# The recurrent branch of a two-layer block on one core: where the projection work stands among its products, and which engine does its elementwise passes

## The chip, the cores and the metric

One core of a Trainium2 chip runs the whole program. The metric is the time of one execution on the device in microseconds: the median of three runs of the kernel before is 2986.39 us (2982.87 to 2990.86).

## The reference

Two layers of a transformer block over 256 context and 256 latent tokens, width 1024. The normed tokens `h` go through one wide projection `w_in`, which feeds three branches and their gates: latent attention, neighbourhood attention, and a recurrence. Layer 0 ends in a dense feed-forward, layer 1 in a mixture of eight experts. The change concerns the recurrence alone, 8 heads of 64, once forward and once backward in time:

```python
w_log = -jax.nn.softplus(-(w0 + jnp.einsum('bldr,drc->bldc', jnp.tanh(wd), w2))) - 0.5
decay = jnp.exp(-jnp.exp(w_log))
a = jax.nn.sigmoid(a0 + jnp.einsum('bldr,drc->bldc', ad, a2))
kk = to_heads(k * k_k, RW_HEADS)
kk = kk / jnp.maximum(jnp.sqrt(jnp.sum(kk * kk, axis=-1, keepdims=True)), 1e-12)
k_dir = k[:, :, None, :] * (1.0 + (a - 1.0) * k_a)
def step(S, inp):
    r_t, w_t, k_t, v_t, kk_t, a_t = inp
    sa = jnp.einsum('bhij,bhj->bhi', S, -kk_t)
    S = S * w_t[:, :, None, :] + sa[..., None] * (kk_t * a_t)[:, :, None, :] + v_t[..., None] * k_t[:, :, None, :]
    return S, jnp.einsum('bhij,bhj->bhi', S, r_t)
bonus = (jnp.sum(r[:, :, None] * k_dir * r_k, axis=-1, keepdims=True) * v[:, :, None]).sum(axis=2)
```

## The kernel before

The projection `w_in` is 57 tiles of up to 128 columns. Each tile is 24 products on TensorE: eight slices of the depth, and for each three products of split operands (`mm3`, L314, L315, L316), 512 tokens wide or 256 where only the latent tokens count. A tile's weights come by DMA, ScalarE rounds them (`whi`, L469) and GpSimd takes the remainder (`wlo`, L470), in two passes of 512 columns for a tile. The generator `serve` gives this work out a slice at a time; the same stream carries the modulation products (L339) of the next layer.

`weave` runs the recurrence and, at each of its `yield w`, draws about `w` microseconds of projection from `serve`. The numbers in `K.W` so say how much projection is laid in at which point. What the recurrence leaves over is drawn later, in the attention. After that a scheduler orders each engine's instructions; each engine then runs its own list in order. The names below are those of the code.

The recurrence of a layer is two halves of four heads, one after the other, each in these steps (`rw_half`):

- **Front** (`rw_front`): the norm of `kk` through two products (L562, L572), a square root on ScalarE and a reciprocal on VectorE. The second half's front stands inside the first half's chain.
- **Preparation**: four rounds (two head pairs, two directions). A round has two products from the low-rank inputs (L609, L614), two tanh and two exponentials on ScalarE, a running sum on VectorE (L620; for the backward direction two further passes, L622 and L623, turn it round), and about ten more VectorE passes that form the operands `KR` and `BK`. After each pair a bonus product on TensorE (L662) takes the result of the last of these passes (L660).
- **Inverse**: products (L684, L686) give the 32 by 32 triangles; 14 steps of substitution on VectorE (L703, L705) and two transposes (L709, L710) invert their parts; then 448 small products on TensorE in three rounds with evictions between them: F (L719), TT and NT (L735, L739), and W and the last corner (L764 to L773).
- **Chain**: eight chunk steps, each needing the state of the one before. On TensorE a step is the state against the keys (L882), eight products of the next chunk (L789), the state carried on (L836, L840), the solve (L892), the new state (L847), a transpose (L821), right sides (L811) and outputs (L858). VectorE and ScalarE evict between them.
- **Output** (`rw_out`): group norm, transposes (L938), gate.

Layer 0's halves run from about 105 to 546 us, layer 1's from 1326 to 1736 us, and the start of layer 1's attention follows.

Of the kernel before, what the change touches and what calls it, by code (L numbers as in the profile page):

```python
# [185 lines left out]
class Kern:  # L186
# [346 lines left out]
    def rw_common(s, l):  # L533
        nc = s.nc
        s.rw_derived(l)
        s.share()
        for tag, n in (("z", 6), ("kk", 2), ("lora", 1), ("kds", 1)):
            s.t([128, T], tag, n)
        s.g2 = s.t([128, 512], "g2", 1)
        nc.sync.dma_start(s.g2, s.I["lora"][l, :, 2])  # L540
        s.m16 = s.t([128, 96], "m16", 1)
        nc.sync.dma_start(s.m16, s.I["cst"][:, KCST:])
        s.wd = s.need("wd")
        nc.scalar.activation(s.wd, s.wd, AF.Tanh)
        s.ad = s.need("ad")
# [5 lines left out]
    def rw_front(s, l, f, t0y):  # L551

        V, A, PE = s.nc.vector, s.nc.scalar, s.nc.tensor
        k = [s.need(f"k{2 * f + i}") for i in range(2)]
        kk = []
        st = s.ps(tag="rw")
        for i in range(2):
            q = s.t([128, T], "kk", 2)
            V.tensor_scalar(q, k[i], s.col(l, "kk", 2 * f + i), None, op0=OP.mult)
            sq = s.tmp()  # L560
            A.activation(sq, q, AF.Square)
            PE.matmul(st[32 * i:32 * i + 32], s.c("hs")[:, 2:], sq, start=True, stop=True)  # L562
            kk.append(q)
        rt = s.tmp()
        A.activation(rt[:64], st[:64], AF.Sqrt)
        yield 1.0
        V.tensor_scalar(rt[:64], rt[:64], 1e-12, None, op0=OP.max)
        V.reciprocal(rt[:64], rt[:64])
        yield 3.0
        for i in range(2):  # L570
            p = s.ps(tag="rw")
            PE.matmul(p, s.c("hst", 128)[32 * i:32 * i + 32], rt[32 * i:32 * i + 32], start=True, stop=True)  # L572
            V.tensor_tensor(kk[i], kk[i], p, OP.mult)
        v = [s.need(f"v{2 * f + i}") for i in range(2)]
        VN = s.piece(2, 1024 * f, 4, 256)
        for j in range(2):
            p = s.ps(tag="rw")
            for u in range(2):
                for i in range(2):
                    tt = 2 * j + u  # L580
                    PE.transpose(p[:, u * 256 + i * 128:u * 256 + i * 128 + 128], v[i][:, tt * 128:tt * 128 + 128], s.id)
            A.activation(VN[:, 2 * j:2 * j + 2, :].rearrange("p a b -> p (a b)"), p, AF.Copy)
            yield 0.5
        r = [s.need(f"r{2 * f + i}") for i in range(2)]
        s.F = k, kk, v, r, VN

    def rw_half(s, l, f, t0y):
# [14 lines left out]
        for i in range(2):  # L602
            hp = 2 * f + i
            kd0 = None
            for d in range(2):
# [21 lines left out]
                A.activation(iP, cum, AF.Exp, scale=-1.0)  # L627
                P8, q8 = c8(P), c8(kk[i])
                e = 0 if d else 63
                for a in (0, 4):  # L630
                    P4 = P8[:, a:a + 4, e:e + 1]
                    V.tensor_tensor(PC[:, a:a + 4, i, d], (P4[:, ::-1] if d else P4).to_broadcast([128, 4, 2]),
                                    s.c("hs")[:, 2:4].unsqueeze(1).to_broadcast([128, 4, 2]), OP.mult)
# [9 lines left out]
                u = s.tmp()  # L643
# [5 lines left out]
                kd = s.t([128, T], "kds", 1) if not d else s.tmp()  # L649
                V.tensor_scalar(kd, ta, s.kc2[l][:, hp:hp + 1], s.kc1[l][:, hp:hp + 1], op0=OP.mult, op1=OP.add)  # L650
                V.tensor_tensor(kd, kd, k[i], OP.mult)
# [7 lines left out]
            u = s.tmp()  # L659
# [51 lines left out]
        yield s.W["solve"] * 4.0  # L711
# [11 lines left out]
        yield s.W["solve"] * 2.0  # L723
# [152 lines left out]
        for n in range(8):  # L876
# [12 lines left out]
            yield s.W["chain"]  # L889
# [6 lines left out]
            yield s.W["chain"]  # L896
            if not last:
                mask(n + 1, 0, nx)
                Hn = end(n, H, st)
                mask(n + 1, 1, nx)  # L900
                values(n + 1, nx)
            if out:
                outputs(n, H, st)
            if not last:
                keys(n + 1, nx)
                right(n + 1, nx)
                H, st = Hn, nx
            yield s.W["chain"]
# [9 lines left out]
    def rw_out(s, l, f, R, t0):  # L918
# [14 lines left out]
        V.tensor_tensor(y, y, st[:, 2, :g].unsqueeze(2).to_broadcast([128, g, 64]), OP.mult)  # L933
        for i in range(2):
# [711 lines left out]
def body(tc, I, O, dbg=None, marks=None):  # L1646
    with ExitStack() as ctx:
# [9 lines left out]
        def rwkv(l, t0):  # L1657
            K.rw_common(l)
            for f in range(2):
# [4 lines left out]
                K.rw_out(l, f, K.R, t0)  # L1664
                yield 1.0

        for l in range(2):
            t0 = 256 * l
            with K.phase(f"o{l}", True, mm=2, md=1):
# [20 lines left out]
                with K.phase(f"rw{l}", rw=5):  # L1690
                    K.W = (dict(prep=5.517, solve=1.0, merge=2.541, chain=1.41, front=1.212, mod=0.976), dict(prep=4.665, solve=1.0, merge=2.178, chain=1.56, front=1.173, mod=0.666))[l]
# [63 lines left out]
```

## Time and profile before

| | |
|---|---|
| median of 3 runs | 2986.39 us |
| the profiled execution | 2989.12 us |
| its span, first to last instruction | 2987.4 us |
| TensorE busy | 2815.1 us, 94% of the span |
| VectorE, ScalarE, GpSimd busy | 64%, 54%, 12% |
| mean granted TensorE clock | 0.957 of full speed |

The span is what the profile covers; the 1.7 us around it belong to the run. Busy time of TensorE is not work at full speed: where the granted clock is below 1.00, the same products take longer and still count as busy.

### The profile page before, as it was taken

Reading aid. Unit: us, or ns where it says so; the run is one execution under the profiler, and the core shown is the slowest. Engines: PE = TensorE matmul, PEld = TensorE weight load, DVE = VectorE, ACT = ScalarE, POOL = GpSimd, SP = SyncE. Lnnn points to the kernel's source line nnn. Section 1 sums busy time; section 2 is a strip of 40 time slices with the busy share of each in tenths; the row PEclk is TensorE's granted clock in tenths of the full one; section 3 lists DMA queues with packets and bytes.
Section 4 is the critical chain, followed back from the end, with each engine's and each line's share of the span. In section 5 each row is a group of like instructions: output and inputs, shape, how many; then the busy total and the mean of one; then the engine's idle time right before and its main releaser. Section 6 shows DMA issues by size and latency. Waiting matters only on the chain. (4 is left out here: it accounts for less than half of the span.)

```text
span 2987.4 us, 48726 instructions
## 1 busy us (share of the span) xinstructions
PE 2815.1 (94%) x19774; PEld 2168.4 (73%) x19774; DVE 1901.3 (64%) x2654; ACT 1621.5 (54%) x2449; POOL 369.9 (12%) x287
## 2 busy tenths in 40 slices
PE   7989979999999999997997979989999999999998
PEld 3566667676777888765766856778878787887876
DVE  4653662527754333267347256779988988888897
ACT  3423423447644332253343436667877777777776
POOL 3221221220010000133233400010000000000000
PEclk9989979999999999998997988989999999999999
DMA  7433311441432333343342333669989999998995
GB/s 273 160 130 103 131 57 61 158 143 57 128 127 80 97 99 104 117 143 110 103 149 95 108 104 109 193 239 361 359 320 363 353 350 342 356 361 335 362 352 205
DMA packets 109016, 582.26 MB, mean 195 GB/s; under 512 B 12912, under 2 KB 26608, under 8 KB 86896
## 3 DMA queue, kind: packets, MB, share of 16 engines
q1 hardware_dynamic: 94640, 557.57, 52.1%
q10 hardware_dynamic: 13632, 19.93, 1.8%
q8 instruction: 157, 2.57, 0.4%
q0 software_dynamic: 512, 1.57, 0.1%
q14 instruction: 75, 0.61, 0.1%
HBM read 554.38 MB, written 24.64 MB: 194 GB/s over the span
## 5 line engine op out<-in xcount | busy, mean ns | idle before, releaser
L314 PE MATMUL pmm<-big,whi 128*128 128x512 f32 (+2 forms) x1392 | 534.4, 385 | 11.1 <-ACT stage L958 3.2
L315 PE MATMUL pmm<-big,whi 128*128 128x512 f32 (+2 forms) x1392 | 517.4, 372 | 7.3 <-DVE big L436 3.6
L316 PE MATMUL pmm<-big,wlo 128*128 128x512 f32 (+2 forms) x1392 | 515.9, 371 | 1.9 <-POOL wlo L470 1.9
L1552 DVE TENSOR_TENSOR mwlo<-share,mwhi 128x1024 fp32r<-128x1024 f32 x398 | 472.2, 1229 | 21.0 <-ACT mwhi L1551 11.7
L1551 ACT ACTIVATE mwhi<-share 128x1024 fp32r<-128x1024 f32 x404 | 423.8, 1059 | 94.2 <-PE pmm L316 68.2
L470 POOL TENSOR_TENSOR wlo<-wraw,whi 128x512 fp32r<-128x512 f32 (+1 forms) x228 | 305.0, 1341 | 721.5 <-ACT whi L469 691.9
L315 PE MATMUL pmm<-mwlo,big 128*128 128x512 f32 x896 | 355.1, 396 | 7.2 <-DVE mwlo L1552 6.7
L314 PEld LDWEIGHTS pmm<-big,whi 128*128 128x128 f32 (+1 forms) x1392 | 267.4, 192 | 117.5 <-issue 37.5
L314 PE MATMUL pmm<-mwhi,big 128*128 128x512 f32 x896 | 352.1, 393 | 0.6 <-ACT big L1439 0.6
L316 PE MATMUL pmm<-mwhi,big 128*128 128x512 f32 x896 | 349.8, 390 | 0.0
L299 DVE TENSOR_TENSOR wlo<-wraw,whi 128x512 fp32r<-128x512 f32 x236 | 158.7, 674 | 252.1 <-ACT whi L298 245.6
L1552 DVE TENSOR_TENSOR mwlo<-mraw,mwhi 128x1024 fp32r<-128x1024 f32 x264 | 310.9, 1223 | 9.1 <-ACT mwhi L1551 3.5
L1551 ACT ACTIVATE mwhi<-mraw 128x1024 fp32r<-128x1024 f32 x264 | 278.0, 1060 | 66.8 <-PE pmm L316 49.8
L315 PEld LDWEIGHTS pmm<-big,whi 128*128 128x128 f32 (+1 forms) x1392 | 267.9, 192 | 55.1 <-DVE big L436 6.0
L316 PEld LDWEIGHTS pmm<-big,wlo 128*128 128x128 f32 (+1 forms) x1392 | 268.1, 193 | 50.6 <-issue 5.1
L298 ACT ACTIVATE whi<-wraw 128x512 fp32r<-128x512 f32 x236 | 145.3, 617 | 288.4 <-PE pmm L315 271.9
L469 ACT ACTIVATE whi<-wraw 128x512 fp32r<-128x512 f32 (+1 forms) x228 | 141.8, 624 | 267.4 <-PE pmm L315 228.3
L315 PEld LDWEIGHTS pmm<-mwlo,big 128*128 128x128 f32 x896 | 168.3, 188 | 48.0 <-DVE mwlo L1552 12.3
L314 PEld LDWEIGHTS pmm<-mwhi,big 128*128 128x128 f32 x896 | 168.3, 188 | 36.3 <-ACT big L1439 1.3
L316 PEld LDWEIGHTS pmm<-mwhi,big 128*128 128x128 f32 x896 | 168.3, 188 | 33.4
L315 PE MATMUL pat<-mwlo,mhh 128*128 128x512 f32 x448 | 175.1, 391 | 1.6 <-DVE mwlo L1552 1.4
L314 PE MATMUL pat<-mwhi,mhh 128*128 128x512 f32 x448 | 174.4, 389 | 0.0
(407 smaller groups left out, 4487.0 us busy)
## 6 DMA issues: line engine op xcount, KB each, us to landing
share<-in_moe SPq DMA_DIRECT2D x100, 2048.0 KB, 9.4
mraw<-in_moe SPq DMA_DIRECT2D x66, 2048.0 KB, 9.5
wraw<-in_win SPq DMA_DIRECT2D x112, 512.0 KB, 3.5
wraw<-in_modw SPq DMA_DIRECT2D x80, 512.0 KB, 4.9
wraw<-in_ffn SPq DMA_DIRECT2D x60, 512.0 KB, 3.5
wraw<-in_wo SPq DMA_DIRECT2D x24, 512.0 KB, 3.8
wraw<-in_wout SPq DMA_DIRECT2D x16, 512.0 KB, 4.6
share<-in_modw SPq DMA_DIRECT2D x12, 512.0 KB, 9.0
```

The costliest lines, as they stand in the source:

```text
L298: nc.scalar.activation(hi, raw[:, a:a + b], AF.Copy)
L299: nc.vector.tensor_tensor(lo, raw[:, a:a + b], hi.bitcast(F32), OP.subtract)
L314: nc.tensor.matmul(out, a[0], b[0], start=first, stop=False)
L315: nc.tensor.matmul(out, a[0], b[1], start=False, stop=False)
L316: nc.tensor.matmul(out, a[1], b[0], start=False, stop=last)
L469: nc.scalar.activation(hi, raw[:, k:k + 4], AF.Copy)
L470: nc.gpsimd.tensor_tensor(lo, raw[:, k:k + 4], hi.bitcast(F32), OP.subtract)
L1551: nc.scalar.activation(hi, raw[:, a:a + 2], AF.Copy)
L1552: (nc.gpsimd if a in pool else nc.vector).tensor_tensor(lo, raw[:, a:a + 2], hi.bitcast(F32), OP.subtract)
```

## The change

- `rw_front`: the sums of squares go to 128 rows and 16 columns (eight narrow products in place of two wide ones, sixteen in place of two to spread the result), so that the root and the reciprocal work on 16 columns and not on 512.
- Preparation: two VectorE passes of each round (the scaling of `lw`, the scaling of `kd`) become ScalarE activations, the backward running sum goes through reversed views in one pass, one narrow pass of two goes in the forward rounds, and temporaries are reused in place. The bonus product and its last pass move into the first two chunk steps.
- Inverse: nothing is drawn between F, TT/NT and W any more; the numbers there move ahead of F. Both halves of W come before both halves of the corner, with one draw between.
- Chain: one draw in a step in place of three, after the solve; masks and transposes stand earlier. The chain's numbers are smaller than their sum was.
- Output: a draw of 5.0 stands between the group norm and its transposes.

```diff
@@ rw_common
+        s.m16 = s.t([128, 97], "m16", 1)
...
+        nc.vector.memset(s.m16[:, 96:97], -0.5 * DEC)
@@ rw_front
-            PE.matmul(st[32 * i:32 * i + 32], s.c("hs")[:, 2:], sq, start=True, stop=True)
+            for tt in range(4):
+                o = 8 * i + 2 * tt
+                PE.matmul(st[:, o:o + 2], sq[:, 128 * tt:128 * tt + 128], s.c("hs")[:, 2:4], start=(o == 0), stop=True,
+                          skip_group_check=True)
...
-        A.activation(rt[:64], st[:64], AF.Sqrt)
-        yield 1.0
...
+        A.activation(rt, st[:, 0:16], AF.Sqrt)
+        V.tensor_scalar(rt, rt, 1e-12, None, op0=OP.max)
+        V.reciprocal(rt, rt)
+        yield 1.5
...
-            PE.matmul(p, s.c("hst", 128)[32 * i:32 * i + 32], rt[32 * i:32 * i + 32], start=True, stop=True)
+            for tt in range(4):
+                o = 8 * i + 2 * tt
+                for hh in range(2):
+                    PE.matmul(p[64 * hh:64 * hh + 64, 128 * tt:128 * tt + 128], rt[:, o + hh:o + hh + 1].to_broadcast([128, 64]), s.id,
+                              start=(tt == 0), stop=True, skip_group_check=True)
@@ rw_half, preparation
-                V.tensor_scalar(lw, lw, -0.5 * DEC, -0.5 * DEC, op0=OP.mult, op1=OP.add)
+                A.activation(lw, lw, AF.Identity, bias=s.m16[:, 96:97], scale=-0.5 * DEC)
...
-                V.tensor_tensor_scan(cum, s.c("scanm"), lw, 0.0, OP.mult, OP.add)
-                if d:
-                    V.tensor_tensor(lw, lw, cum, OP.subtract)
-                    V.tensor_tensor(c8(lw), c8(lw), c8(cum)[:, :, 63:64].to_broadcast([128, 8, 64]), OP.add)
-                    cum = lw
-                P, iP = s.tmp(), s.tmp()
+                rev = (lambda a: a[:, ::-1]) if d else (lambda a: a)
+                V.tensor_tensor_scan(rev(cum), s.c("scanm"), rev(lw), 0.0, OP.mult, OP.add)
+                P, iP = lw, s.tmp()
...
+                A.activation(kd, ta, AF.Identity, bias=s.kc1[l][:, hp:hp + 1], scale=s.kc2[l][:, hp:hp + 1])
+                V.tensor_tensor(kd, kd, k[i], OP.mult)
...
-                for a in (0, 4):
+                for a, b in ((0, 4), (4, 8)) if d else ((0, 8),):
...
-                V.tensor_scalar(kd, ta, s.kc2[l][:, hp:hp + 1], s.kc1[l][:, hp:hp + 1], op0=OP.mult, op1=OP.add)
-                V.tensor_tensor(kd, kd, k[i], OP.mult)
...
-            V.scalar_tensor_tensor(u[:, t0y:], kd0[:, t0y:], s.col(l, "rk", hp), r[i][:, t0y:], op0=OP.mult, op1=OP.mult)
-            pb = s.ps(tag="rw")
-            PE.matmul(pb[:, t0y:], s.c("bd"), u[:, t0y:], start=True, stop=True)
-            V.tensor_tensor(bn[:, t0y:], pb[:, t0y:], v[i][:, t0y:], OP.mult)
+            V.scalar_tensor_tensor(bn[:, t0y:], kd0[:, t0y:], s.col(l, "rk", hp), r[i][:, t0y:], op0=OP.mult, op1=OP.mult)
@@ rw_half, inverse
-        yield s.W["solve"] * 4.0
+        yield s.W["solve"] * 8.0
...
-        yield s.W["solve"] * 2.0
...
-        yield s.W["solve"] * 3.0
...
+            if j:
+                yield s.W["merge"]
...
+        for j in range(2):
             p = s.ps(tag="rw")
...
-            yield s.W["merge"]
@@ rw_half, chunk chain
-            yield s.W["chain"]
+            if not last:
+                mask(n + 1, 0, nx)
...
-            yield s.W["chain"]
             if not last:
-                mask(n + 1, 0, nx)
+                mask(n + 1, 1, nx)
+                keys(n + 1, nx)
+            yield s.W["chain"][f]
+            if not last:
                 Hn = end(n, H, st)
-                mask(n + 1, 1, nx)
...
-            yield s.W["chain"]
+            if n < 2:
+                pb = s.ps(tag="rw")
+                PE.matmul(pb[:, t0y:], s.c("bd"), bonus[n][:, t0y:], start=True, stop=True)
+                V.tensor_tensor(bonus[n][:, t0y:], pb[:, t0y:], v[n][:, t0y:], OP.mult)
@@ rw_out
         V.tensor_tensor(y, y, st[:, 2, :g].unsqueeze(2).to_broadcast([128, g, 64]), OP.mult)
+        yield s.W["out"]
@@ body
-                    K.W = (dict(prep=5.517, solve=1.0, merge=2.541, chain=1.41, front=1.212, mod=0.976), dict(prep=4.665, solve=1.0, merge=2.178, chain=1.56, front=1.173, mod=0.666))[l]
+                    K.W = (dict(prep=5.5, solve=1.1, merge=1.9, chain=(1.9, 1.2), front=1.2, out=5.0, mod=0.976),
+                           dict(prep=4.7, solve=1.1, merge=1.9, chain=(1.9, 1.2), front=1.2, out=5.0, mod=0.666))[l]
```

**TensorE, first half of layer 0, around F.** `pmm` are projection products. Before, from the last projection ahead of F (L719) to the first products behind it:

```order
L316 MATMUL pmm_1346<-big_30_230,wlo_1315 128x512
L719 MATMUL prw_1363<-share_33_290 32x32 x64
L719 MATMUL prw_1429<-share_33_290 32x32 x64
L314 MATMUL pmm_1346<-big_30_230,whi_1347 128x512
L315 MATMUL pmm_1346<-big_31_231,whi_1347 128x512
L316 MATMUL pmm_1346<-big_30_230,wlo_1348 128x512
```

In the changed program, the same place (F is L720 there, TT/NT L735 and L739):

```order
L315 MATMUL pmm_1390<-big_31_231,whi_1391 128x512
L316 MATMUL pmm_1390<-big_30_230,wlo_1392 128x512
L720 MATMUL prw_1417<-share_33_290 32x32 x64
L720 MATMUL prw_1483<-share_33_290 32x32 x64
L735 MATMUL prw_1551<-share_34_291 32x32 x4
L739 MATMUL prw_1552<-share_34_291 32x32 x2
```

Nine projection products stood between F and TT/NT, the first three of them shown; TT/NT now stands right behind F. Counted over the four inverses, 64, 59, 72 and 111 projection products stood between the last triangle product and F, and 102, 102, 132 and 117 stand there now; between F and the chain 49, 33, 45 and 79 stood, and 10, 10, 12 and 23 stand there now.

**TensorE, layer 0, one chunk step.** Before, the last of the six products between the carried state (L836, L840) and the solve (L892):

```order
L314 MATMUL pmm_2201<-big_30_230,whi_2113 128x512
L315 MATMUL pmm_2201<-big_31_231,whi_2113 128x512
L316 MATMUL pmm_2201<-big_30_230,wlo_2114 128x512
L892 MATMUL prw_2238<-rs_2213,share_33_290 64x64
L892 MATMUL prw_2239<-rs_2213,share_33_290 64x64
```

In the changed program, the next chunk's products (L790), the carried state (L837, L841), the solve (L894):

```order
L790 MATMUL prw_2249<-big_127_740,share_32_289 128x128
L837 MATMUL prw_2258<-hst_2217,cst 64x256 x2
L841 MATMUL prw_2258<-hst_2217,big_127_740 64x128 x4
L894 MATMUL prw_2267<-rs_2246,share_33_290 64x64
L894 MATMUL prw_2268<-rs_2246,share_33_290 64x64
```

The six products before the solve are gone; projection stands behind the transposes (L822) that follow the solve, three to nine products in most steps of layer 0. The chains held 209, 190, 293 and 297 projection products and hold 134, 87, 129 and 144.

**TensorE, layer 1, from the last chunk's outputs into the attention.** Before (L858 outputs, L938 transposes, L943 gate, L1303 router, `psc` the attention's own projection):

```order
L858 MATMUL prw_15947<-uv_15902,am_15899 64x64
L938 MATMUL prw_15985<-cst,share_1477_10810 128x128 x2
L943 MATMUL prw_15991<-zl_11260,g_1482_10815 128x256
L938 MATMUL prw_15997<-cst,share_1477_10810 128x128 x2
L943 MATMUL prw_16003<-zl_11260,g_1482_10815 128x256
L1303 MATMUL ptp_16054<-router,mod_2189 128x8 x8
L314 MATMUL psc_16112<-whi_0_16104,yh_16068 128x512
L977 MATMUL ptp_16081<-cst,sq_16065 128x1 x4
L1051 MATMUL ptp_16093<-cst,t_2298_16024 128x32 x4
```

In the changed program, around the router's products (L1309):

```order
L314 MATMUL pmm_15484<-big_1449_10750,whi_15485 128x256
L315 MATMUL pmm_15484<-big_1450_10751,whi_15485 128x256
L316 MATMUL pmm_15484<-big_1449_10750,wlo_15486 128x256
L1309 MATMUL ptp_15444<-router,mod_2417 128x8 x8
L314 MATMUL pmm_15526<-big_1449_10750,whi_15501 128x256
L315 MATMUL pmm_15526<-big_1450_10751,whi_15501 128x256
L316 MATMUL pmm_15526<-big_1449_10750,wlo_15502 128x256
```

Before, no `w_in` projection was left here. In the changed program 432 products of it, 256 wide, stand in layer 1 behind the outputs of the last chunk, 59 of them ahead of L938's place and the others among the first products of the attention.

## Rows read from the trace of the kernel before

**Rows 1.** The page, part 2: TensorE's granted clock in 40 slices of the span, tenths
```profile
PEclk9989979999999999998997988989999999999999
```
**Rows 2.** Busy time by stage: length, then each engine's busy us, PEclk, DMA share, GB/s
```profile
105.00:156.00 51.00, 44.58 (x168) 24.63 (x167) 40.11 (x60) 19.36 (x32) 12.43 (x9) 0.93 0.46 154
156.00:221.00 65.00, 58.46 (x1299) 40.61 (x1299) 35.06 (x54) 18.49 (x35) 14.16 (x11) 0.85 0.35 119
221.00:338.00 117.00, 116.72 (x1113) 80.73 (x1111) 41.88 (x69) 41.76 (x82) 23.02 (x18) 1.00 0.38 127
338.00:389.00 51.00, 41.12 (x170) 26.56 (x170) 43.41 (x62) 19.20 (x33) 16.03 (x12) 0.89 0.26 93
389.00:448.00 59.00, 46.86 (x1231) 39.47 (x1222) 32.58 (x49) 14.67 (x28) 11.13 (x9) 0.75 0.14 45
1326.00:1371.00 45.00, 38.58 (x195) 23.99 (x196) 38.45 (x58) 19.97 (x34) 18.35 (x12) 0.96 0.51 164
1371.00:1434.00 63.00, 52.65 (x1285) 42.32 (x1277) 36.93 (x58) 18.81 (x36) 14.98 (x12) 0.79 0.24 81
1544.00:1592.00 48.00, 38.55 (x187) 26.24 (x185) 41.66 (x62) 19.77 (x35) 20.49 (x14) 0.86 0.42 141
1592.00:1655.00 63.00, 50.34 (x1339) 47.72 (x1338) 34.43 (x48) 20.09 (x41) 21.64 (x17) 0.72 0.26 82
1736.00:1830.00 94.00, 74.54 (x311) 46.68 (x312) 57.80 (x123) 44.60 (x88) 1.42 (x3) 0.71 0.26 81
```
**Rows 3.** Waits of TensorE, both recurrent stretches: who for whom, us, times, longest
```profile
PE prw L662 <- DVE t L660: 29.1, 8, 6.7
PE prw L719 <- DVE share L709: 21.0, 3, 8.7
PE prw L735 <- issue: 10.9, 7, 2.0
PE prw L719 <- issue: 6.5, 4, 2.4
```
**Rows 4.** Waits of TensorE, layer 1, start of the attention
```profile
PE prw L938 <- DVE share L933: 5.9, 1, 5.9
PE ptp L1033 <- DVE N L1018: 5.9, 1, 5.9
```
**Rows 5.** VectorE groups, preparation 338 to 389: count, busy us, mean ns, idle before
```profile
L618 DVE TENSOR_SCALAR t<-t 128x512 f32<-128x512 f32 x4 | 2.8, 694 | 2.0 <-ACT t L612 2.0
L622 DVE TENSOR_TENSOR t<-t,t 128x512 f32<-128x512 f32 x2 | 2.2, 1123 | 0.0
L650 DVE TENSOR_SCALAR t<-t,kc,kc 128x512 f32<-128x512 f32 x2 | 2.0, 1018 | 0.0
```
**Rows 6.** TensorE groups of projection products alone, 533.7 to 543.0
```profile
L314 PE MATMUL pmm<-big,whi 128*128 128x512 f32 x14 | 5.6, 397 | 0.0
```
**Rows 7.** The same, 1599.3 to 1614.0
```profile
L315 PE MATMUL pmm<-big,whi 128*128 128x256 f32 x37 | 11.1, 301 | 0.0
```
**Rows 8.** Timeline of VectorE, preparation: start us, us, operation
```profile
147.76 0.69 DVE L641 TENSOR_TENSOR big<-z,t 128x512 f32<-128x512 f32 x1
148.37 1.77 DVE L644 SCALAR_TENSOR_TENSOR t<-kk,t 128x512 f32<-128x512 f32 x1
```
**Rows 9.** Timeline of GpSimd at the same time
```profile
148.09 1.50 POOL L470 TENSOR_TENSOR wlo<-wraw,whi 128x512 fp32r<-128x512 f32 x1 [3.06 <-ACT whi L469]
```
**Rows 10.** TensorE groups, chunk chain 245.3 to 333
```profile
L789 PE MATMUL prw<-big,share 64*128 64x128 f32 x80 | 5.8, 285 | 0.0
...
L821 PE MATMUL prw<-cst,share 128*128 128x128 f32 x20 | 3.3, 286 | 0.0
...
L572 PE MATMUL prw<-t,cst 32*128 32x512 f32 x4 | 1.1, 640 | 0.0
L562 PE MATMUL prw<-t,cst 128*32 128x512 f32 x4 | 1.1, 604 | 0.0
```
**Rows 11.** Timeline of VectorE within a chunk step
```profile
243.42 0.69 DVE L850 TENSOR_TENSOR hst<-prw,pc 128x512 f32<-128x512 f32 x1 [1.85 <-PE prw L847]
```

More of the change, by code (lines that the diff above doesn't have):

```diff
@@ L540, in rw_common @@
         nc.sync.dma_start(s.g2, s.I["lora"][l, :, 2])
-        s.m16 = s.t([128, 96], "m16", 1)
-        nc.sync.dma_start(s.m16, s.I["cst"][:, KCST:])
+        s.m16 = s.t([128, 97], "m16", 1)
+        nc.sync.dma_start(s.m16[:, 0:96], s.I["cst"][:, KCST:])
+        nc.vector.memset(s.m16[:, 96:97], -0.5 * DEC)
         s.wd = s.need("wd")
@@ L561, in rw_front @@
             A.activation(sq, q, AF.Square)
-            PE.matmul(st[32 * i:32 * i + 32], s.c("hs")[:, 2:], sq, start=True, stop=True)
+            for tt in range(4):
+                o = 8 * i + 2 * tt
+                PE.matmul(st[:, o:o + 2], sq[:, 128 * tt:128 * tt + 128], s.c("hs")[:, 2:4], start=(o == 0), stop=True,
+                          skip_group_check=True)
             kk.append(q)
-        rt = s.tmp()
-        A.activation(rt[:64], st[:64], AF.Sqrt)
-        yield 1.0
-        V.tensor_scalar(rt[:64], rt[:64], 1e-12, None, op0=OP.max)
-        V.reciprocal(rt[:64], rt[:64])
-        yield 3.0
+        rt = s.t([128, 16], "rt", 2)
+        A.activation(rt, st[:, 0:16], AF.Sqrt)
+        V.tensor_scalar(rt, rt, 1e-12, None, op0=OP.max)
+        V.reciprocal(rt, rt)
+        yield 1.5
         for i in range(2):
             p = s.ps(tag="rw")
-            PE.matmul(p, s.c("hst", 128)[32 * i:32 * i + 32], rt[32 * i:32 * i + 32], start=True, stop=True)
+            for tt in range(4):
[3 more added lines that the diff above has]
+                              start=(tt == 0), stop=True, skip_group_check=True)
             V.tensor_tensor(kk[i], kk[i], p, OP.mult)
@@ L617, in rw_half @@
                 A.activation(ta, acc2, AF.Tanh, bias=s.h0[l][:, 8 + 4 * d + hp:9 + 4 * d + hp], scale=0.5)
-                V.tensor_scalar(lw, lw, -0.5 * DEC, -0.5 * DEC, op0=OP.mult, op1=OP.add)
+                A.activation(lw, lw, AF.Identity, bias=s.m16[:, 96:97], scale=-0.5 * DEC)
                 cum = s.tmp()
-                V.tensor_tensor_scan(cum, s.c("scanm"), lw, 0.0, OP.mult, OP.add)
-                if d:
-                    V.tensor_tensor(lw, lw, cum, OP.subtract)
-                    V.tensor_tensor(c8(lw), c8(lw), c8(cum)[:, :, 63:64].to_broadcast([128, 8, 64]), OP.add)
-                    cum = lw
-                P, iP = s.tmp(), s.tmp()
+                rev = (lambda a: a[:, ::-1]) if d else (lambda a: a)
+                V.tensor_tensor_scan(rev(cum), s.c("scanm"), rev(lw), 0.0, OP.mult, OP.add)
+                P, iP = lw, s.tmp()
                 A.activation(P, cum, AF.Exp)
                 A.activation(iP, cum, AF.Exp, scale=-1.0)
+                kd = s.t([128, T], "kds", 1) if not d else cum
+                A.activation(kd, ta, AF.Identity, bias=s.kc1[l][:, hp:hp + 1], scale=s.kc2[l][:, hp:hp + 1])
+                V.tensor_tensor(kd, kd, k[i], OP.mult)
                 P8, q8 = c8(P), c8(kk[i])
                 e = 0 if d else 63
-                for a in (0, 4):
-                    P4 = P8[:, a:a + 4, e:e + 1]
-                    V.tensor_tensor(PC[:, a:a + 4, i, d], (P4[:, ::-1] if d else P4).to_broadcast([128, 4, 2]),
-                                    s.c("hs")[:, 2:4].unsqueeze(1).to_broadcast([128, 4, 2]), OP.mult)
+                for a, b in ((0, 4), (4, 8)) if d else ((0, 8),):
+                    P4 = P8[:, a:b, e:e + 1]
+                    V.tensor_tensor(PC[:, a:b, i, d], (P4[:, ::-1] if d else P4).to_broadcast([128, b - a, 2]),
+                                    s.c("hs")[:, 2:4].unsqueeze(1).to_broadcast([128, b - a, 2]), OP.mult)
                 if d:
@@ L641, in rw_half @@
                 V.tensor_tensor(kr[:, c0:, 1, :], c8(r[i])[:, c0:], P8[:, c0:], OP.mult)
-                u = s.tmp()
+                u = P
                 V.scalar_tensor_tensor(u, kk[i], -0.5, iP, op0=OP.mult, op1=OP.mult)
@@ L648, in rw_half @@
                                        op0=OP.add, op1=OP.mult)
-                kd = s.t([128, T], "kds", 1) if not d else s.tmp()
-                V.tensor_scalar(kd, ta, s.kc2[l][:, hp:hp + 1], s.kc1[l][:, hp:hp + 1], op0=OP.mult, op1=OP.add)
-                V.tensor_tensor(kd, kd, k[i], OP.mult)
                 c42 = lambda a: a.rearrange("p (c x t) -> p c x t", c=4, x=2)
@@ L658, in rw_half @@
                 yield s.W["prep"]
-            u = s.tmp()
-            V.scalar_tensor_tensor(u[:, t0y:], kd0[:, t0y:], s.col(l, "rk", hp), r[i][:, t0y:], op0=OP.mult, op1=OP.mult)
-            pb = s.ps(tag="rw")
-            PE.matmul(pb[:, t0y:], s.c("bd"), u[:, t0y:], start=True, stop=True)
             bn = s.t([128, T], "bonus", 2)
-            V.tensor_tensor(bn[:, t0y:], pb[:, t0y:], v[i][:, t0y:], OP.mult)
+            V.scalar_tensor_tensor(bn[:, t0y:], kd0[:, t0y:], s.col(l, "rk", hp), r[i][:, t0y:], op0=OP.mult, op1=OP.mult)
             bonus.append(bn)
@@ L904, in rw_half @@
             if not last:
-                keys(n + 1, nx)
                 right(n + 1, nx)
                 H, st = Hn, nx
-            yield s.W["chain"]
+            if n < 2:
+                pb = s.ps(tag="rw")
+                PE.matmul(pb[:, t0y:], s.c("bd"), bonus[n][:, t0y:], start=True, stop=True)
+                V.tensor_tensor(bonus[n][:, t0y:], pb[:, t0y:], v[n][:, t0y:], OP.mult)
             if n > 2:
@@ L1663, in rwkv @@
                     K.rw_gate(l, t0)
-                K.rw_out(l, f, K.R, t0)
-                yield 1.0
+                yield from K.rw_out(l, f, K.R, t0)
         for l in range(2):
```

## The prediction

> **What bounds the kernel now.** I read the page first, then TensorE's clock over the span, then the busy times by stage, then TensorE's waits, then single groups.
>
> TensorE is busy for 94% of the span, so the rest of the kernel follows it. The clock's row has its digits below 9 almost only in the first half of the span and near the start of layer 1's attention [rows 1]; the experts behind that run at 9 throughout. The stages show why. In the chunk chain TensorE is busy 116.72 of 117 us at a clock of 1.00. In the four preparations, the four inverses and the start of layer 1's attention it is idle for part of the time and slow for another part [rows 2]. For each of these nine stretches I take as lost its length less busy time times clock, which is the time that the same products would not need if TensorE never waited and stayed at full speed:
>
> - preparations: 51 - 44.58 x 0.93 = 9.5; 51 - 41.12 x 0.89 = 14.4; 45 - 38.58 x 0.96 = 8.0; 48 - 38.55 x 0.86 = 14.8; together 46.7 us
> - inverses: 65 - 58.46 x 0.85 = 15.3; 59 - 46.86 x 0.75 = 23.9; 63 - 52.65 x 0.79 = 21.4; 63 - 50.34 x 0.72 = 26.8; together 87.4 us
> - start of layer 1's attention: 94 - 74.54 x 0.71 = 41.1 us
>
> That is 175.2 us. The projection is the same number of products before and after, so wherever it stands it costs the same at full speed; the time changes only by what of this loss goes or is added. What makes it: eight waits of the bonus product for VectorE, 29.1 us; three waits of F for the substitution's end, 21.0 us; eleven stalls of F and TT/NT that wait for no engine ("issue"), 10.9 + 6.5 = 17.4 us [rows 3]; two waits of 5.9 us for VectorE in the attention [rows 4]; the rest is the halved clock (1.2 for 2.4 GHz) that follows each of these.
>
> **The change part by part.**
>
> *Preparation.* The bonus product leaves it, and with it the place where TensorE's queue stood behind VectorE's last pass of a pair: 29.1 us of waits [rows 3]. The product itself is no cheaper; it stands in the first two chunk steps. What is late next is VectorE's last operand, for which the triangles wait, once in a half and not twice. VectorE was busy 43.41 of 51 us in the second half of layer 0 [rows 2]. The four scalings of `lw` (2.8 us), the two subtractions (2.2) and the scalings of `kd` (2.0 for two) go [rows 5]; L623 and the other two of L650 have the same shapes, so I take 2.5 more: 9.5 us less, about 34 us of passes. TensorE's own work there is 41.12 x 0.89 = 36.6 us; it loses 20 projection products (4.5 us) and two bonus products and gains some modulation, so about 34. VectorE also waits for ScalarE now and then (2.0 us in the row of L618), and its new inputs come from ScalarE, so it ends perhaps 3 us behind TensorE. ScalarE takes over eight passes of a half; it was busy 19.20 of 51 us, which hides them [rows 2]. A backward running sum through reversed views is not in the trace: between nothing and twice the forward sum, off TensorE's path in either case, and I take no difference. I take one wait of 3 us with 3 us of slow clock behind it in each half: 4 x 6 = 24 us in place of 46.7. Bounds: 10 (VectorE in time) and 46 (VectorE as late as now).
>
> *Substitution.* The projection alone costs 9.3 us for 41 products of 512 columns, 0.227 us each (14 in the row, with two fellows of 14 and 13) [rows 6], and 14.7 us for 111 of 256 columns, 0.132 each (three groups of 37) [rows 7]. Ahead of F there now stand 102, 102, 132 (72 wide, 60 narrow) and 117 (81 and 36) products: 23.2, 23.2, 24.3 and 23.1 us, with one to four groups of modulation on top. Before, 64, 59, 72 and 111 stood there. The second to fourth left F waiting for 21.0 us in all; 43 x 0.227 = 9.8 us more in the second, 60 products more in the third, and wider ones in the fourth cover 6.8, 5.5 and 8.7. These waits go.
>
> VectorE's substitution gets longer by this. A pass of 512 columns took 0.69 us, and the next, of the same kind, 1.77 us [rows 8]; a GpSimd pass of the projection ran from 148.09 for 1.50 us beside the second [rows 9]. Twelve products need one such pass, so the substitutions get about 3, 4, 5 and 1 more of them, at 1.1 us each up to 5.5 us. The 24 us of projection have about that in hand. The Trainium skill, "SBUF — State Buffer", section "Who interferes with whom", says that a VectorE instruction with two SBUF inputs and a GpSimd instruction that reads SBUF exclude each other for the whole instruction. The trace agrees in kind (1.77 for 0.69 us); by the full 1.50 us a pass, the third substitution would gain 7.5 us and not 5.5. That is the first rival below.
>
> *Inverse products.* F, TT/NT, W and the corner now follow each other with 10, 10, 12 and 23 projection products among them, where 49, 33, 45 and 79 stood. The evictions are short against them, but the stalls without a releaser were there even with projection between: 17.4 us in eleven, 1.58 us each [rows 3], that is just under three in a half. With nothing between them I take six in a half, 9.5 us, and 3 us of slow clock: 12.5 a half, 50 us in place of 87.4 for substitution and products together. Bounds: 35 (as few stalls as now) and 85 (F still waits, and more stalls). The Trainium skill, "Runtime: NRT & Kernel Launch", section "Instruction fetch mechanics", says that instructions come in blocks of 256 and that crossing into the next is mostly hidden; by that the stalls would not be seen at all, and the sum would be 38 us lower. The trace speaks against it here, with 10.9 us in seven stalls on L735 alone.
>
> *Chain.* It loses 495 products of 512 or 256 columns in four halves, which is no gain by itself: TensorE had no idle time there, and they are paid elsewhere. What must hold is that the step does not become bound by its own waits. In the 117 us of eight steps VectorE was busy 41.88 and ScalarE 41.76 us [rows 2], 5.2 us a step each. TensorE keeps 116.72 - 75 x 0.227 = 99.7 us, 12.5 a step, with the front in it. VectorE waited 1.85 us for TensorE before the new state's pass of 0.69 us [rows 11]. So I take no loss.
>
> *Start of layer 1's attention.* 432 products, 57 us at 0.132, now stand where TensorE lost 41.1 us; before the router's products alone stand 59 + 13 of them, 9.5 us, against a wait of 5.9 [rows 4]. The stretch's own work is 52.9 us, so it becomes one of 110 us and more, with TensorE as its bound. VectorE had 57.80 us there, and 36 GpSimd passes beside it add up to 36 x 1.1 = 40. I take a loss of 14 us (waits that the projection does not stand before). Bounds: 5 and 41.
>
> *Front.* Four times, two wide products (L562, 1.1 us for a front) become eight of 128 x 128 weights and two columns, and two (L572, 1.1 us) become sixteen of 128 columns; in the trace each such product has two passes. Their nearest rows are 0.165 us (3.3 / 20) and 0.073 us (5.8 / 80) [rows 10]: 16 x 0.165 + 32 x 0.073 = 4.9 us in place of 2.2, so 2.7 more, 10.8 us in all. Bounds: 5 with 0.073 throughout, 23 with 0.165; a gain is excluded, since TensorE's queue has no wait there. VectorE's passes over 512 columns that go cost nothing now.
>
> **The sum.** Preparation 24 - 46.7 = -22.7; inverse 50 - 87.4 = -37.4; attention 14 - 41.1 = -27.1; front +10.8. Together -76.4 us. The profiled execution took 2989.1 us (span 2987.4 and 1.7 around it), 2.7 above the median, which is within the spread of the three runs: 2989.1 - 76.4 = 2912.7, forecast **2913 us**. Its own range is 2870 to 2940: with the lower bounds throughout, 46.7 - 10 + 87.4 - 35 + 41.1 - 5 - 5 = 120 us, 2869; 2940 if the terms come out a third smaller.
>
> **Rivals.**
>
> - *GpSimd makes VectorE the bound.* The projection that covers the substitution and fills the attention brings its passes beside VectorE's. If each costs VectorE its whole 1.5 us, F waits again (inverses 64 and not 50) and the attention's start, 57.8 + 36 x 1.5 = 112 us of VectorE, keeps some 30 us of loss. Sum: -22.7 - 23.4 - 11.1 + 10.8 = -46.4, **2943 us**. For it: the 1.77 us [rows 8]. Against it: not every pass meets a pass with two SBUF inputs.
> - *The idle time only moves.* If the stalls behind F double again (another 38 us) and the preparation's wait stays as long as now (+22.7), 61 of the 76 us go: **2974 us** or a little more. For it: VectorE is the late engine in every preparation.
> - *The chain becomes bound by its own waits.* With three to nine projection products in a step, the way state, right side, eviction, solve, eviction, new state, eviction is less covered, and ScalarE's queue holds the projection's rounding between two of its evictions, so that a late GpSimd pass holds up the step. There are 32 steps; from 76.4 / 32 = 2.4 us lost in each it decides, and at 3 us (96 us) the time is 2989.1 - 76.4 + 96 = **3009 us**, slower. Against it: 5.2 us of VectorE and of ScalarE in a step of 12.5.
>
> **How the numbers follow.** Forecast 0.63, GpSimd 0.20, idle moved 0.07, chain 0.07, and 0.03 for more than 120 us gained. A measurement of this kernel tells about 0.3%, 9 us, from no change. Faster: 0.63 + 0.20 + 0.03 + most of the 0.07 that lies at 2974 = 0.88; the rest of that case, same 0.05; slower 0.07. The range of 8 in 10 reaches from 2870 over the GpSimd case to 2966; outside stay the last two rivals and the best case.
>
> **What the profile after would show.** Preparations: one wait of about 3 us before the triangles and none for the bonus. Substitution: F without a wait for VectorE, or below 2 us. Inverse: about six stalls a half before TT/NT, W and the corner. Chain: TensorE busy throughout at clock 1.00 in steps of less than 13 us. Attention of layer 1: clock of 0.9 or more from 1736 us on in the old count. The forecast is wrong if F still waits 5 us and more for VectorE, if the chain shows idle time of more than 1 us a step, or if the attention's start still runs at 0.7.

## The result and the profile after

The changed kernel takes 2903.89 us (median of four runs, 2897.75 to 2909.30), 0.9719 of the kernel before (95% interval 0.9692 to 0.9746): 84 us faster, forecast 76. The profiled executions are 2989.12 and 2897.75 us, 91.4 us apart, so terms read from the traces add up to 91, not 84.

TensorE's clock first, the same row as [rows 1]:

```profile
PEclk9989989999999999999998999899999999999999
```

The digit 7 is gone. The stages that answer to [rows 2], same columns: preparation, inverse and chunk chain of layer 0's halves, preparation and inverse of layer 1's, start of its attention.

```profile
106.00:143.00 37.00, 37.00 (x162) 21.38 (x165) 28.87 (x42) 23.46 (x39) 11.55 (x8) 1.00 0.51 167
143.00:211.00 68.00, 57.33 (x1319) 42.94 (x1319) 37.44 (x57) 19.19 (x36) 15.19 (x12) 0.82 0.44 145
211.00:300.00 89.00, 88.66 (x1017) 66.03 (x1015) 37.82 (x68) 34.24 (x71) 13.43 (x11) 1.00 0.23 74
303.00:338.00 35.00, 35.00 (x145) 20.66 (x144) 30.12 (x39) 22.04 (x36) 11.92 (x10) 1.00 0.61 208
338.00:398.00 60.00, 50.31 (x1289) 42.99 (x1287) 35.13 (x56) 17.39 (x33) 16.46 (x12) 0.83 0.22 76
398.00:465.00 67.00, 66.35 (x875) 51.75 (x875) 30.40 (x49) 27.19 (x58) 7.67 (x6) 1.00 0.24 76
1290.00:1321.00 31.00, 31.00 (x153) 18.14 (x154) 26.29 (x37) 22.14 (x39) 10.98 (x8) 1.00 0.54 173
1321.00:1391.00 70.00, 54.01 (x1334) 45.90 (x1326) 42.30 (x63) 20.27 (x39) 17.98 (x14) 0.83 0.30 101
1468.00:1509.00 41.00, 38.63 (x190) 25.12 (x192) 32.72 (x42) 24.27 (x42) 18.00 (x14) 0.88 0.55 175
1509.00:1572.00 63.00, 52.11 (x1332) 44.63 (x1328) 33.37 (x53) 18.71 (x36) 17.50 (x14) 0.84 0.34 114
1631.00:1741.00 110.00, 99.96 (x661) 81.88 (x659) 62.52 (x116) 61.90 (x132) 41.90 (x34) 0.97 0.48 152
```

By the forecast's measure (length less busy time times clock) three preparations lose nothing now and the fourth 41 - 38.63 x 0.88 = 7.0 us; the inverses lose 21.0, 18.2, 25.2 and 19.2, together 83.6; the attention's start loses 110 - 99.96 x 0.97 = 13.0. The gain is in the preparations and the attention. The inverses, from which most was expected, lost 87.4 before and lose 83.6 now.

TensorE's waits in both recurrent stretches, as in [rows 3]:

```profile
PE prw L735 <- issue: 13.0, 8, 3.1
PE prw L685 <- issue: 7.6, 3, 3.4
PE prw L720 <- issue: 6.8, 3, 2.8
PE prw L739 <- issue: 6.4, 4, 2.1
PE pmm L314 <- DVE z L512: 4.0, 1, 4.0
...
PE ptp L1039 <- DVE N L1024: 2.8, 2, 2.2
```

No wait of the bonus product or of F (L720) for VectorE is left. Stalls without a releaser take their place: with the smaller rows of L687, L764, L765 and L774 they are 24, 41.0 us in all; counted the same way, 14 with 20.4 us before.

A second account does without the clock: for each recorded product the time by which it moves TensorE's end on, and the idle time just before it, summed by kind over the whole trace (us):

```
                              before         after       change
bonus product               10.8 + 29.1     6.7 +  0.0   -33.1
F                           14.2 + 27.5     9.8 +  6.8   -25.2
projection, all split ones  2105.6 + 35.9  2085.6 + 38.2 -17.7
attention's own products   223.7 + 13.7   205.8 +  7.6  -24.1
output and gate              9.7 +  7.0     8.2 +  0.4    -8.1
triangles                   26.7 +  0.6    17.2 + 10.1     0.0
W and corner                19.4 +  0.0    20.8 +  4.8    +6.2
TT/NT                       24.4 + 13.3    28.9 + 19.4   +10.6
front                       13.9 +  0.0    19.3 +  0.0    +5.4
```

The small rest (chunk chain -3.0, modulation -2.1, the preparation's products +1.0 and others) brings it to -91. The attention's row is both layers', without its share of the split products. F's gain and what TT/NT, W and the corner lose nearly cancel each other.

### The profile page after: what moved, and what is told of

It is laid out like the page before. It is cut to its first block, busy times and chain, and to the rows that moved or that the text cites. A ratio compares the mean times of both kernels' runs of the same rounds, so it can differ in the third digit from the quotient of the medians.

```text
span 2896.0 us, 49048 instructions
## 1 busy us (share of the span) xinstructions
PE 2762.0 (95%) x19934; PEld 2161.8 (75%) x19934; DVE 1867.1 (64%) x2600; ACT 1635.2 (56%) x2479; POOL 369.8 (13%) x287
## 5 line engine op out<-in xcount | busy, mean ns | idle before, releaser
L314 PE MATMUL pmm<-big,whi 128*128 128x512 f32 (+2 forms) x1392 | 531.0, 382 | 14.7 <-DVE z L512 4.0
L316 PEld LDWEIGHTS pmm<-mwhi,big 128*128 128x128 f32 x896 | 168.3, 188 | 33.4
```

The source lines that it names most:

```text
L314: nc.tensor.matmul(out, a[0], b[0], start=first, stop=False)
L316: nc.tensor.matmul(out, a[1], b[0], start=False, stop=last)
```

## The experiments

Each ratio is to the kernel before, with its 95% interval; the change itself is 0.9719.

**The bonus product alone (kernel before).** It is taken out of the preparation (`bn` becomes the product of kd0, rk and r) and added to the chunk step:

```diff
+            if n < 2:
+                pb = s.ps(tag="rw")
+                PE.matmul(pb[:, t0y:], s.c("bd"), bonus[n][:, t0y:], start=True, stop=True)
+                V.tensor_tensor(bonus[n][:, t0y:], pb[:, t0y:], v[n][:, t0y:], OP.mult)
```

> The kernel before with one edit: the bonus product goes from the preparation into the first two chunk steps. Theory (TensorE's queue stood behind VectorE there): the eight waits of 29.1 us go, VectorE still ends some 5 us behind TensorE in each preparation, so about 25 us of the 88 between the two kernels, 2963 us. Rival (the wait only moves to the triangles, since VectorE has the same passes to make): within 9 us of the kernel before, with a wait of 6 us or more in front of the triangles in three of the four preparations.

0.9870 (0.9854 to 0.9887), 39 us: the largest single part. TensorE's waits:

```profile
PE prw L680 <- DVE share L646: 12.9, 3, 5.4
PE prw L715 <- DVE share L705: 9.1, 3, 4.2
```

The 29.1 us became 12.9 us in front of the triangles, three waits as the rival said, but the time fell as the theory said, and by more: the projection that no longer stands in the preparation stands ahead of F (75 products for 59 in the second half), whose waits fell from 21.0 to 9.1 us.

**The order alone (kernel before).** The table of weights, the places of `yield` and the new chunk step:

```diff
-        yield s.W["solve"] * 4.0
+        yield s.W["solve"] * 8.0
...
-        yield s.W["solve"] * 2.0
...
-        yield s.W["solve"] * 3.0
```

> The kernel before with the new order alone: weights, places where the projection is drawn, order of the chunk step; the preparation and the bonus product stay. Theory: F's waits (21.0 us) go and the start of layer 1's attention loses about 13 us and not 41, while the bonus waits and the inverse products' stalls stay: about 45 us faster, 2944 us. Rival (the order is worth something only with a shorter preparation): under 20 us faster.

0.9921 (0.9903 to 0.9940), 24 us, nearer to the rival. The bonus waits stayed at 26.8 us. F's waits for VectorE went, and the stalls went up to 19 with 27.0 us.

**The new passes alone (kernel before).** The expectation names the new front too, but the kernel of this run keeps the old one, and so does that of the next run.

```diff
-                V.tensor_scalar(lw, lw, -0.5 * DEC, -0.5 * DEC, op0=OP.mult, op1=OP.add)
+                A.activation(lw, lw, AF.Identity, bias=s.m16[:, 96:97], scale=-0.5 * DEC)
...
+                V.tensor_tensor_scan(rev(cum), s.c("scanm"), rev(lw), 0.0, OP.mult, OP.add)
```

> The kernel before with the new passes of the preparation and the new front alone; bonus product and order stay. Theory: the preparation's end is set by VectorE, each half has some 9 us less of it, so the bonus waits shrink from 29.1 us to under 10 and the time by about 25 us, 2964 us. Rival (VectorE's passes are off the path and only the product's place counts): under 9 us faster. With the theory the three parts together give more than the 84 us measured, because passes and bonus product take away the same wait.

0.9978 (0.9969 to 0.9988), 7 us: the rival. The bonus waits fell from 29.1 to 21.0 us only. Each bonus product still stands behind VectorE's last pass of its pair; why the shorter passes took no more of the wait away is not shown.

**Bonus product and new passes together, in the old order.** The edits of the first and the third run in one kernel; the front is the old one.

> The kernel before with the late bonus product and the new passes and front, in the old order. Alone these gave 39 and 6 us. Theory (with the bonus product out of the way TensorE's queue stands at the triangles behind VectorE, 12.9 us in three waits, and the shorter passes take that away): more than the sum, 55 to 65 us, 2925 to 2932, with preparations at full clock and no wait before the triangles. Rival (the two add up): 45 us, 2943.

0.9838 (0.9824 to 0.9852), 48 us; the sum of the two alone is 39 + 7 = 46. They add up, as the rival said; my theory of a larger joint gain is not borne out, though the waits in front of the triangles fell from 12.9 to 5.5 us. Nor do the three parts alone give more than the 84 us, as I had written before the passes' run: 39 + 24 + 7 = 70. What is left to the order and the new front, on top of these two, is 0.9838 - 0.9719 = 0.0119, 36 us. The last run below finds no gain by the front, so the order is the larger part of it.

**No projection for layer 1's attention (kernel after).**

```diff
-                           dict(prep=4.7, solve=1.1, merge=1.9, chain=(1.9, 1.2), ...
+                           dict(prep=4.7, solve=1.1, merge=1.9, chain=(5.2, 5.2), ...
```

> The kernel after, with layer 1's chunk chains drawing so much that no projection is left for layer 1's attention (layer 0 unchanged). Theory (the attention's start was short of work for TensorE): its loss goes from 13 us back to about 41, the time to some 2930 us. Rival (the attention was helped by something else, such as its own order or the clock it starts with): within 9 us of after.

0.9809 (0.9773 to 0.9845), 27 us slower than after, as the theory said. The start of the attention, and its waits:

```profile
1684.00:1794.00 110.00, 96.25 (x440) 59.83 (x440) 73.93 (x169) 60.28 (x123) 1.42 (x3) 0.77 0.21 65
```
```profile
PE prw L944 <- DVE share L938: 6.3, 2, 5.9
...
PE ptp L1039 <- DVE N L1024: 6.4, 2, 5.8
```

It loses 110 - 96.25 x 0.77 = 35.9 us for 13.0, and the two waits of 5.9 us of [rows 4] are back (5.9 and 5.8). The two losses are 22.9 us apart. So most of the order's 36 us is this; the 27 us themselves have intervals of about 10 us.

**The old places around the substitution (kernel after).** The three lines of the order's diff above, turned round.

> The kernel after, with the projection around the substitution drawn where the kernel before drew it: half ahead of F, the rest between F, TT/NT and W. Theory of the forecast (cover and stalls are exchanged for each other): F waits for VectorE again, three times and about 15 us in all, the stalls fall from 24 to about 12 and from 41 to some 20 us, so the time is within 10 us of after. Rival (F's cover is what was gained, the stalls are no dearer without projection between): 20 to 30 us slower, 2925 to 2935.

0.9719 (0.9699 to 0.9739), the same as after. The stalls fell to 16 with 33.4 us, less than expected; F waited only 0.9 us for VectorE. Ahead of it in layer 0 stood 81 products of 512 columns, fewer than the 102 of after but more than the 64 and 59 of the kernel before:

```profile
PE prw L720 <- issue: 11.4, 4, 3.9
PE prw L736 <- issue: 8.8, 5, 2.7
...
PE prw L720 <- DVE share L710: 0.9, 1, 0.9
```

The theory holds in its result, not in its 15 us of waits. Beside the other edits, the last 21 of the 102 products under the substitution are worth nothing measurable; the cover of the kernel before is not what this run tests.

**F twice (kernel after).** `for j in range(2)` becomes `for j in (0, 0, 1, 1)`. The first result of each pair is not unread, as the expectation has it: VectorE evicts it (L722, 16 passes for 8) and then evicts the second over it. TensorE waited for none of these passes.

> The kernel after, with the F products made twice, the first time into a bank that nothing reads; 256 recorded products more in each half. Theory (stalls go by the number of instructions): 2.4 us of products and two more stalls of about 2 us in each half, with slow clock behind them: 25 to 35 us more than after, 2930 to 2940, and some 32 stalls in place of 24. Rival (a stall belongs to the change from one group of products to the next): 4 x 2.4 = 10 us more, 2914, and 24 to 25 stalls.

0.9825 (0.9802 to 0.9848), 32 us slower than after, and exactly 32 stalls, 52.1 us:

```profile
PE prw L720 <- issue: 21.5, 11, 2.8
PE prw L735 <- issue: 9.9, 8, 1.7
```

Eight more, all at F (eleven for three), whose 1024 recorded products are doubled: one more stall for each 128. They go by the number of instructions and not by the place. In the trace after, a timeline of TensorE around F and TT/NT shows the beat (start, us, operation, and the idle time before it):

```profile
186.00 0.91 PE L720 MATMUL prw<-share 32*32 32x32 f32 x86 [1.78 <-issue]
...
189.73 0.26 PE L735 MATMUL prw<-share 32*32 32x32 f32 x2 [2.36 <-issue]
...
193.46 0.32 PE L735 MATMUL prw<-share 32*32 32x32 f32 x6 [1.17 <-issue]
...
197.19 0.26 PE L739 MATMUL prw<-share 32*32 32x32 f32 x2 [1.27 <-issue]
```

They are 3.73 us apart each time, with 128 recorded products between two of them; each has its weight load, so these are 256 instructions. 128 of F's take 1.2 us at full clock, 128 of TT/NT's 2.5 us at half; the rest of the 3.73 is the stall.

The DMA queues show what arrives at this beat. One queue carries instructions, in packets of 16384 bytes (third part of the pages, after and then F twice: packets, MB, share):

```profile
q8 instruction: 158, 2.59, 0.4%
```
```profile
q8 instruction: 166, 2.72, 0.4%
```

Eight packets more came with 1024 products, 1024 weight loads and eight stalls more: 256 instructions for a packet and for a stall. In the trace after, the packets of the stretch above start at 183.59, 187.12, 190.99, 194.60 and 198.33 us and take 1.0 to 1.2 us each; every one of the 24 stalls ends 1.2 to 1.5 us after the end of such a packet, and every one of the 32 in F twice 1.1 to 1.6 us. So the stalls are TensorE's wait for its next packet of instructions.

**Projection inside the runs of small products (kernel after).** In the triangles, F, TT/NT, W and the corner, here for F; layer 1's `chain` becomes (0.6, 0.2):

```diff
+                if q % 4 == 3:
+                    yield s.W["mix"]
```

> The kernel after, with projection drawn inside the runs of small products (one group of three after each 16 to 18 of the triangles, F, TT/NT, W and corner products), and the chain of layer 1 given less of it. Theory (the stalls without a releaser are instructions that arrive too late for products of 9 to 20 ns, about 3.5 us for each 128 recorded products): with 10 us of projection more in each half the 24 stalls of 41.0 us fall below 10, TensorE's clock in the inverses rises from 0.82-0.84 to above 0.95, and the loss there from 83.6 us to under 40: about 2860 us. Rival (a stall belongs to the place, as the first after an eviction, and comes whatever stands between): some 20 stalls stay, the time is 2895 to 2915. Rival (the chain starves with less projection in it): chain steps with idle time of over 1 us, slower than after.

0.9689 (0.9663 to 0.9714), about 9 us less than after, which is within the intervals. The mechanism is as the theory has it, the time is not: the inverses run at full clock in layer 0, and 4 stalls with 8.1 us are left (6.6 of them one stall), but layer 1's attention had spent its projection (behind the router's products 144 of it were left, for 360 in after):

```profile
142.00:225.00 83.00, 81.49 (x1415) 54.19 (x1407) 41.09 (x65) 25.31 (x46) 24.10 (x20) 1.00 0.49 167
348.00:421.00 73.00, 73.00 (x1372) 53.47 (x1360) 36.69 (x54) 24.61 (x45) 25.97 (x21) 1.00 0.29 100
...
1636.00:1746.00 110.00, 100.03 (x504) 73.03 (x502) 68.60 (x133) 59.70 (x121) 18.23 (x15) 0.78 0.33 105
```

**The same in layer 0 alone, with fewer draws** (one for two in the triangles, W and the corner; `mix=0.0` in layer 1).

> The kernel after, with projection inside the runs of small products in layer 0 only (one group of three after each 12 products of F's 16, TT/NT's 18; one or two in the triangles, W and the corner); layer 1 as in after. From the two runs read so far: with mixing in both layers, layer 0 ended 14.7 us earlier than in after and layer 1 lost 12.7 us of that, since its attention ran out of projection. Theory (the loss in layer 1 is that shortage): layer 0's gain stays, 2904 - 15 = 2889, or 2885 with the smaller number of draws. Rival (the gain of layer 0 is taken back by its attention, which gets less projection): 2900 or more.

0.9668 (0.9645 to 0.9691), median 2890.21: layer 0's gain stays. The loss of its inverses went from 39.2 to 2 us, yet layer 1's first preparation began only 20.7 us earlier (1268.95 for 1289.64). A timeline of this kernel shows one price:

```profile
375.48 0.50 PE L314 MATMUL pmm<-big,whi 128*128 128x512 f32 x1
375.81 0.40 PE L315 MATMUL pmm<-big,whi 128*128 128x512 f32 x1
376.05 0.39 PE L316 MATMUL pmm<-big,wlo 128*128 128x512 f32 x1
376.37 0.45 PE L721 MATMUL prw<-share 32*32 32x32 f32 x32
```

Three projection products and the switch take 376.37 - 375.48 = 0.89 us here, and 0.68 by [rows 6].

**In both layers, and no draws in layer 1's chunk steps** (`mix=0.6`, `chain=(0.0, 0.0)`, `out=2.0` there).

> The same mixing in both layers, and no projection drawn in layer 1's chunk chains, so that its attention keeps about as much as in after (324 products of 256 columns against 336). Theory (chains need no cover, inverses and attention do): layer 1 gains too, some 20 us of its 44 us of loss in the inverses: 2865 to 2880. Rival (the chain without projection becomes bound by its own waits, from 1 us a step): 16 steps, so that layer 1 loses 15 us or more against mixing in layer 0 alone.

0.9648 (0.9627 to 0.9670), median 2880.57, faster than both kernels. Its lead over the run before is within the intervals, so layer 1's part is not shown. Layer 1's two inverses lose 17.2 and 8.4 us here by the forecast's measure, for 25.2 and 19.2 in after, and its attention 14.6 for 13.0:

```profile
1303.00:1382.00 79.00, 71.07 (x1415) 56.38 (x1414) 42.33 (x66) 24.79 (x46) 25.80 (x20) 0.87 0.41 137
1479.00:1561.00 82.00, 78.33 (x1497) 64.46 (x1497) 41.19 (x63) 31.00 (x60) 37.87 (x29) 0.94 0.48 157
1612.00:1722.00 110.00, 100.46 (x656) 80.74 (x655) 65.35 (x123) 63.25 (x134) 39.63 (x31) 0.95 0.45 143
```

The chunk chain did not starve: 0.4 us idle over its last 50 us.

**The old front (kernel after).** The wide products of L562 and L572 [rows 10] in place of the narrow ones, with the old draws between them.

> The kernel after with the old front (wide products over 512 columns). As forecast (the narrow products cost 10.8 us more on TensorE): about 11 us faster than after, 0.968 of the kernel before. By the trace after, in which the two lines of products together take no longer than before: within 3 us of after, 0.971 to 0.973; and if VectorE's passes over 512 columns are on the path again, slower than after.

0.9733 (0.9711 to 0.9755): not told apart from after, and not the 11 us faster of the forecast. TensorE's groups in the first chunk chain, after and then with the old front:

```profile
L579 PE MATMUL prw<-cst,rt 128*64 128x128 f32 x32 | 2.3, 276 | 0.0
...
L566 PE MATMUL prw<-cst,t 128*128 128x2 f32 x16 | 1.9, 252 | 0.0
```
```profile
L573 PE MATMUL prw<-t,cst 32*128 32x512 f32 x4 | 2.2, 640 | 0.0
L563 PE MATMUL prw<-t,cst 128*32 128x512 f32 x4 | 2.1, 605 | 0.0
```

In the same surroundings both forms take the same time; over the whole trace, by the second account, the fronts take 17.6 us in the old form and 19.3 in the new.

## Why the prediction was right in the sum and wrong in a term

- **Preparation** (24 us forecast, 7.0 measured). Right in kind: no bonus wait. Too careful in size: the wait of 3 us before the triangles did not come in any half. VectorE was busy 30.12 of 35 us in the second half, where 43.41 of 51 stood.
- **Substitution.** F waits no more, as forecast, and the runs bear out the reason given, projection ahead of it. By the forecast's prices it came to 13.4 to 14.7 us in a half before, with 21.0 us of waits; to 16.3 to 19.4 in the two runs with the late bonus product in the old order, with 9.1 and 9.0; to 18.4 to 19.5 with the old places in the kernel after, with 0.9; and to 23.1 to 24.3 in after, with none. The new passes made no difference to F between the 9.1 and the 9.0. The forecast longer substitution did not come: from the first to the last transposition it took 21.7, 23.1, 24.2 and 22.7 us for 21.0, 22.6, 23.6 and 24.8, with 5, 8, 7 and 7 GpSimd passes started beside it for 5, 5, 6 and 9. I had counted 3, 4, 5 and 1 more; it was 0, 3, 1 and 2 fewer. So neither price of a pass was put to the test in the time, and the rule quoted from the Trainium skill, "SBUF — State Buffer", "Who interferes with whom", is not decided here.
- **Inverse products: the step that failed** ("six in a half, 9.5 us, and 3 us of slow clock"). The stalls are right, 24 with 41.0 us for 24 with 38. The slow clock is not: of 83.6 us, 41.0 are stalls and 5.4 a wait of the projection (4.0) and one of the modulation (1.4), so 37 us in four halves are clock, 9 a half and not 3. No row stood behind the 3: busy time less busy time times clock in [rows 2] gives 8.8, 11.7, 11.1 and 14.1 us for the four inverses before. Behind the stalls the granted clock stood at 0.53 for 11.9 us and at 0.50, the lower of its two levels (1.2 for 2.4 GHz), for 3.9 in the first half:

```profile
186.70:198.60 11.90, 7.10 (x405) 6.71 (x394) 2.70 (x4) 1.65 (x3) 1.89 (x2) 0.53 0.02 6
198.60:202.50 3.90, 3.15 (x86) 2.80 (x79) 2.35 (x4) 2.24 (x4) 0.00 (x0) 0.50 0.03 6
```

  The gain of 37.4 us became 3.8. The beat of 256 instructions agrees with the block that the Trainium skill names in "Runtime: NRT & Kernel Launch", "Instruction fetch mechanics"; "mostly hidden" does not hold for products this short, with 41.0 us in 24 stalls.
- **Attention** (14 forecast, 13.0 measured): right, and the run without projection there bears it out.
- **Front** (+10.8 forecast, +5.4 in the account): the lower bound. The duration came from rows of small products in long runs of their own kind. Of the 5.4 only 1.8 go with the form, as the run with the old front shows.
- **Chain**: right. Eight steps take 89 us with the front and 67 without, 11.1 and 8.4 each, at clock 1.00, TensorE busy 88.66 and 66.35 us. The forecast had 12.5 with the front; part of the difference is modulation that left the chain too (L339, 8.7 us of it before and 4.3 after).
- **What the sum lacked.** The terms measured give -39.7 - 3.8 - 28.1 + 5.4 = -66 us of 91. Part of the rest is seen, not explained to the end: by the second account the projection's 1221 products of 512 columns that run from 91 to 662 us before took 308.0 us, and the same ones, from 92 to 625 us, 297.0 after. In the first half's chunk steps, in groups between small products, they cost 0.26 us each before (216 in 55.8) and 0.25 after (135 in 33.1); in groups of 24 under the substitution 0.24 (5.67 us for 24), and 0.227 in the long run of [rows 6]. Both the measure and the forecast took a product for equally dear wherever it stands. The measure also counts a small product at half clock as half its time. How much of the rest each of these makes stays open.

So the sum came within 8 us by luck: an error of 34 us in the inverses met 17 in the preparations, 5 in the front and the unforecast rest. The likeliest case held as a time and in three of its mechanisms, not in its largest term. Of the rivals, "the idle time only moves" describes the inverses, and nothing else.

## What to carry over

Look first for a product that stands in TensorE's queue behind another engine's last pass, and move that product: here it was worth more than shortening the passes or covering the wait. Where long runs of very short products stall without a releaser, count instructions against the packets that bring them, set other work between them, and count the slow clock behind the stalls at its measured length. Work that fills gaps is a stock: each place that draws more of it empties another, and it costs more in small portions.

## What the runs showed of the hardware

- Short products come at a beat: 3.73 us for 128 recorded products with their weight loads, seen three times in a row, and 3.45 to 4.02 elsewhere, while the products themselves took 1.2 to 2.5 us. A packet of 16384 bytes of instructions, 256 of them, comes once in each beat. With projection between (128 in four portions of 1.27 us, 5.1 us) the stall is gone.
- Keeping the clock up has a price of its own: a portion of three projection products between small ones took 0.89 us, and 0.68 in a long run.
